# A hybrid decoder layer on one core: sums with one operand in PSUM, and twelve blocks stored alike

## The chip, the cores and the metric

The kernel runs on one core of one Trainium2 chip. The metric is the device time of one execution in microseconds; the median of three runs is given. A core has five engines that work side by side, each with a queue of its own that keeps its order: TensorE (matmuls), VectorE and ScalarE (element by element), GpSimd, and SyncE, called SP here, which issues the transfers (DMAs). [...]

## The reference

One decoder layer on x of 1024 tokens by 1024 channels, all in float32:

```python
h = rms_norm(x, norm_pre_mix)
mix = hybrid_mixer(h, ...)              # RWKV-7 heads beside a causal convolution
x = x + rms_norm(mix, norm_post_mix)
h = rms_norm(x, norm_pre_ffn)
hid = causal_dwconv(h @ ffn_up, ffn_conv_w, ffn_conv_b)   # 3 taps; 1024 -> 2 x 2816
gate, up = hid[..., :2816], hid[..., 2816:]
f = (gelu(gate) * up) @ ffn_down                           # 2816 -> 1024
out = x + rms_norm(f, norm_post_ffn)
```

The change lies in the part from `h @ ffn_up` to the product of gelu(gate) and up.

## The kernel before

The tokens are worked on in two halves of 512. A product of matrices keeps float32's accuracy by splitting both operands into a high part (a rounded copy) and a low part (the rest), and adding three matmuls: high x high, high x low, low x high. For a weight of 128 x 512 ScalarE casts the high part (`wh`), and GpSimd subtracts to get the low part (`wl`); both happen in `split`, line 162. Two buffers each hold `wh` and `wl`, three hold the raw weight (`wr`).

The 2816 channels of the feed-forward part are 22 blocks of 128, each with a gate and an up branch. `project` makes one branch of one block and half of the tokens: 24 matmuls with two weights into one PSUM bank. `taps` applies the three taps of the convolution: ScalarE's scaled copy (line 887) and two VectorE instructions that read the bank and add to an SBUF tile (line 896). `ffn_pair` makes both branches, gelu (line 906) and the product (line 908).

The work goes in this order:

- The mixer, for both halves. Beside its end the first 12 blocks of the first half are made (`EARLY`). They must be kept until the down projection, so they go to DRAM (`early`). Of the 12, the first 8 (`KEPT`) are held in `row` tiles of SBUF, two blocks a tile, and the text stores them at the head of the feed-forward part (line 1196); the last 4 are stored from `pt` tiles where they are made (line 1371).
- `gates`: the gate branches of the last 10 blocks (`JOINT`) of the first half, with the second half's normalisation beside them.
- The plain pairs (lines 1204 to 1206): the first 12 blocks (`PLAIN`) of the second half, one `ffn_pair` each, the result stored to `plain`. `beside` puts next to each pair one step of `weight_sums` (four GpSimd sums, line 1041, with their loads and stores) and one step of `act_sums`, which makes sums and differences of the two halves' activations: four rounds of two steps.
- The joint blocks (`shared`, lines 1210 and 1211): the last 10 blocks for both halves, in a scheme that needs five products in place of six and uses those sums.
- `ffn_down`, the down projection, by a similar scheme with seven products in place of eight, and the output.

From the feed-forward part on, six PSUM banks are handed out in turn (`self.bank()`); two more have the tags "pn" and "pn2" and serve the normalisation and, at the end, the down projection. Within `act_sums` three SBUF tiles x, y and z of the pool `f2p` (six tiles) hold the sums of a round.

The order of each engine's queue is not written by hand: a planner simulates the kernel and puts the instructions in order by priority and readiness. Weight loads, splits and taps are marked high priority. `beside` adds the rule that on VectorE, GpSimd and SP the extra steps come behind the pair's product, its last low part and its last weight load.

Of the kernel before, what the change touches and what calls it, by code (L numbers as in the profile page):

```python
# [13 lines left out]
F32 = mybir.dt.float32  # L14
F32R = mybir.dt.float32r
BF16 = mybir.dt.bfloat16
AF = mybir.ActivationFunctionType
ALU = mybir.AluOpType
# [4 lines left out]
P = 128  # L23
SEQ = 1024
D = 1024
KT = D // P
HALF = 512
# [11 lines left out]
FT = D_FF // P  # L39
# [10 lines left out]
BUFS = {"v": 2, "gd": 1, "pt": 6, "kk": 1, "l8": 5, "ca": 6, "ck": 6, "r": 2,  # L50
        "mixr": 1, "co": 4, "po": 1, "c": 4, "t2": 2}

EARLY, KEPT = 12, 8

JOINT = 10
PLAIN = FT - JOINT
# [42 lines left out]
class Trunk:  # L99
# [181 lines left out]
    def pair(self, what, pool):  # L281
        return tuple(pool.tile([P, HALF], F32R, tag="h", name=self.nm(what)) for _ in range(2))
# [534 lines left out]
    def setup_ffn(self, ctx):  # L817
        nc, tc = self.nc, self.tc
        pool = lambda name, bufs=1: ctx.enter_context(tc.tile_pool(name=name, bufs=bufs))
        cp = pool("fconst")  # L820

        self.turn = cycle([lambda: self.xs[0], lambda: self.xs[1]]
                          + [lambda t=t: Trunk.bank(self, t) for t in ("pe", "pe", "pb", "pb")])
        self.bank = lambda tag="pb": self.Y if tag == "pn2" else Trunk.bank(self, "pc") if tag == "pn" else next(self.turn)()
        self.nrowp = pool("nrowp")

        self.ap = pool("actp", 2 * (FT - KT) - KEPT)
        self.h1p = pool("h1p", 2 * KT)
        self.tp = pool("tp", 8)
        self.f2p = pool("f2p", 6)  # L830
        self.post_ffn = cp.tile([P, D], F32, name="post_ffn")
        nc.sync.dma_start(self.post_ffn, self.a["post_ffn"].broadcast_to([P, D]))
        self.fcarry = cp.tile([P, 2, FT, 2], F32, name="fcarry")
        self.fss = cp.tile([P, 8, 2], F32, name="fss")
# [63 lines left out]
    def ffn_pair(self, h, hs, i, temp, out=None):  # L898

        nc = self.nc  # L900
        accs = []
        for br in range(2):
            ps = self.project(self.a["ffn_up"][br * FT + i], P, hs)
            accs.append(temp())
            self.taps(h, i, br, ps, accs[br])
        nc.scalar.activation(accs[0], accs[0], AF.Gelu_apprx_tanh)
        out = accs[0] if out is None else out
        self.gated = nc.vector.tensor_tensor(out, accs[0], accs[1], ALU.mult)
        return out

    def beside(self, *parts):
# [46 lines left out]
    def act_sums(self, h0, h1, S):  # L958

        nc = self.nc  # L960
        f = lambda t: t.bitcast(F32)
        add = lambda o, x, y: nc.vector.tensor_tensor(o, x, y, ALU.add)
        sub = lambda o, x, y: nc.vector.tensor_tensor(o, x, y, ALU.subtract)

        def pair(n, hi, lo, src):
            self.split(hi, lo, src)
            S[n].append((hi, lo))

        for k in range(4):
            a11, a12, a21, a22 = h0[k], h0[4 + k], h1[k], h1[4 + k]  # L970
            two = [p.tile([P, D], F32R, tag=t, bufs=4, name=self.nm("s")) for p, t in ((self.nrowp, "nrow"), (self.rowp, "row"))]
            x, y, z = (self.f2p.tile([P, HALF], F32, tag="f2", name=self.nm("r")) for _ in range(3))
            whole = lambda out, a: add(out, f(a[0]), f(a[1]))
            whole(z, a11)
            whole(x, a21)
            sub(z, z, x)
            pair(3, *a11, z)
            whole(y, a22)
            add(x, x, y)
            pair(1, two[0][:, :512], two[0][:, 512:], x)  # L980
            yield
            sub(y, y, z)
            pair(2, two[1][:, :512], two[1][:, 512:], y)
            whole(z, a12)
            sub(z, z, y)
            pair(4, *a12, z)
            yield

    def shared(self, i, S, A22, act0, act1, raws):

        nc = self.nc
        temp = lambda: self.f2p.tile([P, HALF], F32, tag="f2", name=self.nm("acc"))
        kview = lambda t: t.rearrange("p (k m) -> p k m", k=4)
        up = self.a["ffn_up"]

        def add(out, x, y):
            with self.tc.high_priority():
                nc.vector.tensor_tensor(out, x, y, ALU.add)

        if raws is None:  # L1000
            T = lambda n: self.weight(kview(self.usums[n - 1]), [P, 4, P])
            b22 = lambda: self.weight(up[FT + i, 1], [P, 4, P])
        else:
            with self.tc.high_priority():
                b11, b12, b21, b22r = raws
                for n in (1, 3, 0, 2):
                    self.load = nc.sync.dma_start(kview(raws[n]), up[n % 2 * FT + i, n // 2])
                t3 = self.wp.tile([P, HALF], F32, tag="wr", bufs=3, name=self.nm("t3"))
                self.four_sums(b11, b12, b21, b22r, t3)

            def pair(raw):
                with self.tc.high_priority():
                    hi, lo = (self.wp.tile([P, HALF], F32R, tag=t, bufs=2, name=self.nm(t)) for t in ("wh", "wl"))
                    self.low = self.split(hi, lo, raw, True)[1]
                return kview(hi), kview(lo)

            T = lambda n: pair((b12, b11, t3, b21)[n - 1])
            b22 = lambda: pair(b22r)
        x, y, z = (self.bank() for _ in range(3))
        self.four(x, T(2), S[2], True, True)  # L1020
        add(act1, act1, x)
        self.four(y, T(1), S[1], True, True)
        W = temp()
        add(W, act1, y)
        self.four(z, T(3), S[3], True, True)
        add(x, W, z)
        self.four(y, b22(), S[4], False, True)
        add(y, act1, y)
        self.four(z, T(4), A22, False, True)
        add(z, act1, z)  # L1030
        two = [temp() for _ in range(2)]
        self.taps(0, i, 1, y, two[0])
        nc.vector.tensor_tensor(act0, act0, two[0], ALU.mult)
        self.taps(1, i, 0, z, act1)
        nc.scalar.activation(act1, act1, AF.Gelu_apprx_tanh)
        self.taps(1, i, 1, x, two[1])
        nc.vector.tensor_tensor(act1, act1, two[1], ALU.mult)

    def four_sums(self, b11, b12, b21, b22, t3):

# [138 lines left out]
    def run(self):  # L1179
        nc = self.nc  # L1180
        self.setup()
        sts = [{}, {}]
        with ExitStack() as ctx:
            self.setup_mixer(ctx)
            h0, early = self.mixer(sts)
        with ExitStack() as ctx:
            self.setup_ffn(ctx)
            h1 = []
# [3 lines left out]
            sums = self.weight_sums()  # L1192
            temp = lambda: self.f2p.tile([P, HALF], F32, tag="f2", name=self.nm("acc"))
            act = lambda: self.ap.tile([P, HALF], F32, tag="act", name=self.nm("act"))
            for i, e in enumerate(early[:KEPT]):
                nc.sync.dma_start(self.early[i], e)
            one = [self.ffn_pair(0, h0, i, temp, act()) for i in range(EARLY, PLAIN)]
            both = [[act() for _ in range(JOINT)] for _ in range(2)]
            turn = cycle((True, False))
# [3 lines left out]
            ss = self.act_sums(h0, h1, S)  # L1203
            for i in range(PLAIN):
                nc.sync.dma_start(self.plain[i], self.ffn_pair(1, h1, i, temp))
                self.beside(sums, ss)
            list(ss)
            list(sums)
            raws = [self.h1p.tile([P, HALF], F32, tag="h", name=self.nm("b")) for _ in range(8)]
            for n, i in enumerate(range(PLAIN, FT)):  # L1210
                self.shared(i, S, h1[4:], both[0][n], both[1][n], raws[n % 2 * 4:n % 2 * 4 + 4] if n else None)
            kept = []
            for i in range(0, KEPT, 2):
                two = self.row("row", 4)
                nc.sync.dma_start(two.rearrange("p (i t) -> p i t", i=2), self.early[i:i + 2].rearrange("i p t -> p i t"))
                kept += [two[:, :HALF], two[:, HALF:]]
            back = [self.hp.tile([P, HALF], F32, tag="h", name=self.nm("act")) for _ in range(2 * KT)]
            for i in range(KEPT, EARLY):
                nc.sync.dma_start(back[PLAIN + i - KEPT], self.early[i])
            for i in range(PLAIN):  # L1220
                nc.sync.dma_start(back[i], self.plain[i])
            acts = [kept + back[PLAIN:] + one + both[0], back[:PLAIN] + both[1]]
# [2 lines left out]
    def mixer(self, sts):  # L1225
        nc, tc = self.nc, self.tc
# [84 lines left out]
        with self.stream("norm"):  # L1311
            two = [self.tl("l8", [P, 2, D]) for _ in range(2)]
# [3 lines left out]
            hs = self.pairs("h")  # L1316
# [21 lines left out]
        hs = self.pairs("h")  # L1338
# [23 lines left out]
        conv(1, 2, W[3].mark)  # L1362
        conv(1, 3)
        conv_norm(1)
        early = []
        with self.stream("proj"):
            piece = lambda: self.tl("pt", [P, HALF])
            for i in range(EARLY):
                if i >= KEPT:
                    early.append(self.early[i])  # L1370
                    nc.sync.dma_start(early[-1], self.ffn_pair(0, h0, i, piece))
                    continue
                if i % 2 == 0:
                    two = self.row("row", 4)
                early.append(self.ffn_pair(0, h0, i, piece, two[:, i % 2 * HALF:(i % 2 + 1) * HALF]))
        prepare(4)
        with self.stream("proj"):
            self.w_out(1, mixes[1], [sts[1]["co", i] for i in range(4)], W[3].merged)
        return h0, early


def pack(ins):
# [70 lines left out]
```

## Time and profile before

| | |
|---|---|
| median of three runs | 1309.98 us (1307.91 to 1310.06) |
| profiled execution | 1311.76 us |
| its span | 1310.0 us |
| TensorE (PE) busy | 1242.8 us, 95% of the span |
| VectorE (DVE) busy | 923.4 us, 70% |
| ScalarE (ACT) busy | 721.5 us, 55% |
| GpSimd (POOL) busy | 508.2 us, 39% |
| granted TensorE clock, mean | 0.979 of full speed |

The span is the time from the first to the last instruction that the profiler saw on the core. Busy shares are means over stages with different limits: a stage's own limit is read from the windows of that stage. [...]

### The profile page before, as it was taken

To read this page: it belongs to the slowest core of one execution; us is meant where nothing else is said; L and a number is where in the kernel's file an instruction comes from. 1 tells how busy PE (TensorE), PEld (TensorE's weight loads), DVE (VectorE), ACT (ScalarE), POOL (GpSimd) and SP (SyncE) were. 2 spreads that over 40 slices of the span, in tenths; PEclk is the share of its full clock that TensorE was granted. 3 is DMA by queue.
4 is the path that set the end of the run, shared out by engine and by line. 5 is a ranking of instruction groups with operands and counts; after the bars stand their busy time and mean duration, and the time that the engine had idled before them with its cause. 6 is when DMAs were issued, how large, how long until landed. Compare 5 with 4: busy or idle time off the path is not lost.

```text
span 1310.0 us, 23010 instructions
## 1 busy us (share of the span) xinstructions
PE 1242.8 (95%) x8460; PEld 998.3 (76%) x8460; DVE 923.4 (70%) x1540; ACT 721.5 (55%) x1490; POOL 508.2 (39%) x438
## 2 busy tenths in 40 slices
PE   6999989999999989999999999889999999999996
PEld 5777767787779867778799777666877888888885
DVE  5276998996689979996520556776366768479567
ACT  6563664657655755557642475545545555544451
POOL 4443420110113422444464388887588860000001
PEclk9999989999999979999999999998999999999998
DMA  7554433343333451332354777676522236335326
GB/s 237 166 153 129 130 98 102 95 140 111 115 112 106 127 172 35 97 89 82 113 155 140 256 267 272 233 250 220 173 57 73 81 120 218 97 105 163 110 65 209
DMA packets 105505, 185.70 MB, mean 142 GB/s; under 512 B 15184, under 2 KB 21712, under 8 KB 105392
## 3 DMA queue, kind: packets, MB, share of 16 engines
q1 hardware_dynamic: 105392, 184.23, 44.1%
q8 instruction: 67, 1.10, 0.3%
q14 instruction: 46, 0.38, 0.1%
HBM read 141.58 MB, written 42.60 MB: 141 GB/s over the span
## 4 chain that ended last, share of the span: by engine, by line
PE 54%; DVE 7%; POOL 4%; DMA 3%; issue 3%; ACT 2%; SPq 0%; POOLq 0%; ACTq 0%
PE pb L135 24%; PE pe L135 14%; PE xs L135 11%; POOL b L1041 2%; DVE pc L416 2%; PE Y L135 2%; PE pc L135 2%; POOL wl L162 2%; DMA wr<-ffn_up 1%; DMA x<-x1d 1%; DVE nrow L1096 1%; DMA nrow<-x 1%; PE pc L150 1%; DVE x L1080 0%; DMA pt<-mixd 0%
## 5 line engine op out<-in xcount | busy, mean ns | idle before, releaser
L162 POOL TENSOR_TENSOR wl<-wr,wh 128x512 fp32r<-128x512 f32 (+1 forms) x181 | 244.5, 1352 | 262.4 <-ACT wh L162 233.6
L162 ACT CAST wh<-wr 128x512 fp32r<-128x512 f32 (+1 forms) x220 | 135.2, 615 | 180.3 <-issue 43.9
L135 PE MATMUL pb<-h,wh 128*128 128x512 f32 (+3 forms) x720 | 229.5, 398 | 2.5 <-ACT wh L162 1.0
L135 PE MATMUL pb<-f,wh 128*128 128x512 f32 x584 | 186.3, 399 | 4.4 <-ACT wh L162 3.3
L416 DVE SCALAR_TENSOR_TENSOR pc<-c,params,pc 128x512 f32<-128x512 f32 x232 | 174.2, 751 | 8.1 <-ACT pc L413 4.1
L135 PEld LDWEIGHTS pb<-h,wh 128*128 128x128 f32 (+2 forms) x720 | 131.7, 188 | 35.1 <-ACT wh L162 2.7
L135 PE MATMUL pb<-h,wl 128*128 128x512 f32 (+3 forms) x360 | 146.3, 406 | 2.2 <-POOL wl L162 2.1
L135 PEld LDWEIGHTS pb<-f,wh 128*128 128x128 f32 x584 | 109.7, 190 | 29.7 <-ACT wh L162 4.8
L135 PE MATMUL pb<-f,wl 128*128 128x512 f32 x292 | 117.6, 403 | 3.2 <-POOL wl L162 3.2
L135 PE MATMUL pe<-f,wh 128*128 128x512 f32 x312 | 99.8, 401 | 2.9 <-ACT wh L162 2.8
L157 POOL TENSOR_TENSOR ss<-var,mhalf 128x1 f32<-128x1 f32 x16 | 11.0, 693 | 227.6 <-DVE ss L1077 202.7
L1041 POOL TENSOR_TENSOR b<-b,b 128x512 f32<-128x512 f32 x66 | 92.9, 1410 | 3.3 <-DMA b<-ffn_down 1.9
L135 PE MATMUL xs<-f,wh 128*128 128x512 f32 x272 | 86.8, 401 | 2.5 <-ACT wh L162 2.1
L135 PEld LDWEIGHTS pb<-h,wl 128*128 128x128 f32 (+2 forms) x360 | 67.6, 188 | 20.6 <-POOL wl L162 4.4
L135 PEld LDWEIGHTS pe<-f,wh 128*128 128x128 f32 x312 | 59.5, 192 | 17.0 <-ACT wh L162 4.0
L135 PEld LDWEIGHTS pb<-f,wl 128*128 128x128 f32 x292 | 55.7, 191 | 17.5 <-POOL wl L162 5.7
L135 PE MATMUL pe<-f,wl 128*128 128x512 f32 x156 | 63.4, 407 | 2.6 <-POOL wl L162 2.6
L135 PEld LDWEIGHTS xs<-f,wh 128*128 128x128 f32 x272 | 51.5, 191 | 14.8 <-ACT wh L162 2.5
L896 DVE SCALAR_TENSOR_TENSOR pt<-pb,params,pt 128x511 f32<-128x511 f32 (+1 forms) x48 | 35.7, 744 | 31.7 <-ACT ecarry L889 31.2
L135 PE MATMUL xs<-f,wl 128*128 128x512 f32 x136 | 54.6, 401 | 1.9 <-POOL wl L162 1.9
L162 POOL TENSOR_TENSOR wl<-b,wh 128x512 fp32r<-128x512 f32 x36 | 47.0, 1306 | 22.4 <-ACT wh L162 18.6
L706 POOL TENSOR_TENSOR XG<-r,GE 64x256 f32<-64x256 f32 x30 | 20.5, 685 | 88.5 <-DVE r L725 83.7
(402 smaller groups left out, 2901.9 us busy)
## 6 DMA issues: line engine op xcount, KB each, us to landing
wr<-ffn_up SPq DMA_DIRECT2D x117, 256.0 KB, 2.8
wr<-w_in SPq DMA_DIRECT2D x80, 256.0 KB, 2.9
b<-ffn_down SPq DMA_DIRECT2D x44, 256.0 KB, 4.4
sums<-b SPq DMA_DIRECT2D x44, 256.0 KB, 2.8
wr<-sums SPq DMA_DIRECT2D x44, 256.0 KB, 2.7
lows<-wl SPq DMA_DIRECT2D x40, 256.0 KB, 3.3
wl<-lows SPq DMA_DIRECT2D x40, 256.0 KB, 2.7
b<-ffn_up SPq DMA_DIRECT2D x40, 256.0 KB, 2.7
```

Of the source, the lines that this page charges most:

```text
L135: return self.nc.tensor.matmul(out, lhsT, rhs, start=start, stop=stop, skip_group_check=skip)
L150: self.nc.tensor.transpose(out, in_, self.con("ident")[:n, :n])
L157: self.nc.gpsimd.tensor_tensor(out, v[:, :n], self.mhalf[:, :n], ALU.pow)
L162: return self.nc.scalar.copy(hi, src), eng.tensor_tensor(lo, src, hi.bitcast(F32), ALU.subtract)
L416: nc.vector.scalar_tensor_tensor(out, c[:, j:j + HALF], w(j), acc, ALU.mult, ALU.add)
L706: nc.gpsimd.tensor_tensor(x[64:128], R[64:128, gs], w.GE[64:128, c, gs].unsqueeze(2).broadcast_to([64, 4, CH]), ALU.mult)
L896: nc.vector.scalar_tensor_tensor(acc[:, o:], ps[:, :HALF - o], w(j), acc[:, o:], ALU.mult, ALU.add)
L1041: sub = lambda o, x, y, op=ALU.subtract: self.nc.gpsimd.tensor_tensor(o, x, y, op)
L1096: nc.vector.tensor_tensor(out, a, b, op)
```

## The change

In `act_sums` the tiles x, y and z become PSUM banks: the two tagged ones and one in turn, and a second one in turn for the last sum of a round. A whole sum (high part plus low part) is now a ScalarE copy of the low part into the bank and a VectorE addition of the high part to it. Where two sums are joined, ScalarE first copies one out of PSUM to an `f2p` tile. So no VectorE instruction here has two inputs in SBUF. A round has three steps in place of two, and every third plain pair gets two steps. In `ffn_pair` of the second half, and at the end of `shared`, gelu writes to a PSUM bank that was already tapped, and the product reads it there. The mixer's twelve blocks are all written to `row` tiles and stored in the mixer, each right behind its product in the text; `KEPT` goes. The pool `actp` keeps 20 tiles.

```diff
-EARLY, KEPT = 12, 8
+EARLY = 12
...
-        self.ap = pool("actp", 2 * (FT - KT) - KEPT)
+        self.ap = pool("actp", 2 * JOINT)
...
     def ffn_pair(self, h, hs, i, temp, out=None):
-        accs = []
+        pss, accs = [], []
         for br in range(2):
-            ps = self.project(self.a["ffn_up"][br * FT + i], P, hs)
+            pss.append(self.project(self.a["ffn_up"][br * FT + i], P, hs))
             accs.append(temp())
-            self.taps(h, i, br, ps, accs[br])
-        nc.scalar.activation(accs[0], accs[0], AF.Gelu_apprx_tanh)
+            self.taps(h, i, br, pss[br], accs[br])
+        gate = pss[0] if h else accs[0]
+        nc.scalar.activation(gate, accs[0], AF.Gelu_apprx_tanh)
         out = accs[0] if out is None else out
-        self.gated = nc.vector.tensor_tensor(out, accs[0], accs[1], ALU.mult)
+        self.gated = nc.vector.tensor_tensor(out, gate, accs[1], ALU.mult)
...
-            x, y, z = (self.f2p.tile([P, HALF], F32, tag="f2", name=self.nm("r")) for _ in range(3))
-            whole = lambda out, a: add(out, f(a[0]), f(a[1]))
+            def whole(out, a):
+                nc.scalar.copy(out, f(a[1]))
+                add(out, f(a[0]), out)
+
+            def copy(src):
+                r = self.f2p.tile([P, HALF], F32, tag="f2", name=self.nm("r"))
+                nc.scalar.copy(r, src)
+                return r
+
+            x, y, z = self.bank("pn"), self.bank("pn2"), self.bank()
             whole(z, a11)
             whole(x, a21)
-            sub(z, z, x)
+            r = copy(x)
+            sub(z, z, r)
             pair(3, *a11, z)
             whole(y, a22)
-            add(x, x, y)
+            add(x, r, y)
+            sub(y, y, copy(z))
+            yield
             pair(1, two[0][:, :512], two[0][:, 512:], x)
+            pair(2, two[1][:, :512], two[1][:, 512:], y)
             yield
-            sub(y, y, z)
-            pair(2, two[1][:, :512], two[1][:, 512:], y)
+            z = self.bank()
             whole(z, a12)
-            sub(z, z, y)
+            sub(z, z, copy(y))
             pair(4, *a12, z)
             yield
...
         self.taps(1, i, 0, z, act1)
-        nc.scalar.activation(act1, act1, AF.Gelu_apprx_tanh)
+        nc.scalar.activation(z, act1, AF.Gelu_apprx_tanh)
         self.taps(1, i, 1, x, two[1])
-        nc.vector.tensor_tensor(act1, act1, two[1], ALU.mult)
+        nc.vector.tensor_tensor(act1, z, two[1], ALU.mult)
...
-            for i, e in enumerate(early[:KEPT]):
-                nc.sync.dma_start(self.early[i], e)
...
                 nc.sync.dma_start(self.plain[i], self.ffn_pair(1, h1, i, temp))
-                self.beside(sums, ss)
+                self.beside(sums, *[ss] * (2 if i % 3 == 0 else 1))
...
             for i in range(EARLY):
-                if i >= KEPT:
-                    early.append(self.early[i])
-                    nc.sync.dma_start(early[-1], self.ffn_pair(0, h0, i, piece))
-                    continue
                 if i % 2 == 0:
                     two = self.row("row", 4)
-                early.append(self.ffn_pair(0, h0, i, piece, two[:, i % 2 * HALF:(i % 2 + 1) * HALF]))
+                nc.sync.dma_start(self.early[i], self.ffn_pair(0, h0, i, piece, two[:, i % 2 * HALF:(i % 2 + 1) * HALF]))
```

## Rows read from the trace of the kernel before

**Rows 1.** The page: busy time by engine, and the chain that ended last.

```profile
PE 1242.8 (95%) x8460; PEld 998.3 (76%) x8460; DVE 923.4 (70%) x1540; ACT 721.5 (55%) x1490; POOL 508.2 (39%) x438
...
PE 54%; DVE 7%; POOL 4%; DMA 3%; issue 3%; ACT 2%; SPq 0%; POOLq 0%; ACTq 0%
```

**Rows 2.** Windows: length, busy us and instructions by engine, clock, DMA share, GB/s.

```profile
784.90:806.70 21.80, 21.80 (x94) 17.47 (x94) 11.83 (x13) 11.72 (x25) 18.07 (x14) 1.00 0.80 270
806.70:907.50 100.80, 88.18 (x339) 66.65 (x338) 76.99 (x80) 53.34 (x109) 82.55 (x58) 0.93 0.69 240
907.50:941.50 34.00, 33.98 (x145) 27.04 (x144) 13.56 (x15) 19.07 (x40) 18.79 (x15) 1.00 0.51 160
...
765.00:780.00 15.00, 15.00 (x74) 12.34 (x73) 8.66 (x17) 9.09 (x21) 12.44 (x11) 1.00 0.90 317
971.00:1085.00 114.00, 113.96 (x490) 91.25 (x489) 79.41 (x112) 65.35 (x138) 87.68 (x67) 1.00 0.32 100
```

**Rows 3.** TensorE's timeline at the start of pair 4: start, us, instructions, wait.

```profile
836.16 0.73 PE L135 MATMUL xs<-f,wh 128*128 128x512 f32 x2 [2.11 <-ACT wh L162]
...
838.05 0.99 PE L135 MATMUL xs<-f,wh 128*128 128x512 f32 x2
...
842.38 0.64 PE L135 MATMUL xs<-f,wh 128*128 128x512 f32 x2
```

**Rows 4.** GpSimd: low halves before and after 806.7 us (ns min/median/max), two timeline rows.

```profile
L162 POOL TENSOR_TENSOR wl<-wr,wh x8: 1288/1306/1737, 783.4 to 802.0; 128x512 fp32r<-128x512 f32 x8
...
L162 POOL TENSOR_TENSOR wl<-wr,wh x29: 1256/1463/1790, 807.8 to 906.6; 128x512 fp32r<-128x512 f32 x29
...
791.99 2.67 POOL L1041 TENSOR_TENSOR b<-b,b 128x512 f32<-128x512 f32 x2
...
818.30 3.44 POOL L1041 TENSOR_TENSOR b<-b,b 128x512 f32<-128x512 f32 x2
```

**Rows 5.** VectorE's groups with both inputs in SBUF: busy us, mean ns, idle before.

```profile
L962 DVE TENSOR_TENSOR r<-f,f 128x512 f32<-128x512 f32 x16 | 22.1, 1418 | 0.1
...
L908 DVE TENSOR_TENSOR acc<-acc,acc 128x512 f32<-128x512 f32 x12 | 14.3, 1195 | 1.2
L963 DVE TENSOR_TENSOR r<-r,r 128x512 f32<-128x512 f32 x12 | 13.7, 1140 | 0.0
...
L1037 DVE TENSOR_TENSOR act<-act,acc 128x512 f32<-128x512 f32 x10 | 11.6, 1162 | 1.8 <-ACT act L1035 1.8
...
L162 DVE TENSOR_TENSOR f<-r,f 128x512 fp32r<-128x512 f32 x8 | 8.3, 1032 | 0.0
...
L962 DVE TENSOR_TENSOR r<-r,r 128x512 f32<-128x512 f32 x4 | 6.7, 1668 | 0.1
...
L162 DVE TENSOR_TENSOR s<-r,s 128x512 fp32r<-128x512 f32 x8 | 5.8, 731 | 0.0
```

**Rows 6.** VectorE: line 896 from 806 to 907 us, and groups of lines 1096 and 998.

```profile
L896 DVE SCALAR_TENSOR_TENSOR acc<-xs,params,acc x12: 734/748/751, 806.4 to 896.8; 128x511 f32<-128x511 f32 x6, 128x510 f32<-128x510 f32 x6
...
L1096 DVE TENSOR_TENSOR act<-act,act 128x512 f32<-128x512 f32 x17 | 11.3, 691 | 0.0
...
L998 DVE TENSOR_TENSOR pe<-act,pe 128x512 f32<-128x512 f32 x10 | 6.9, 690 | 8.1 <-PE pe L135 8.1
```

**Rows 7.** ScalarE's groups: SBUF to SBUF, PSUM to SBUF, SBUF to PSUM.

```profile
L162 ACT CAST wh<-wr 128x512 fp32r<-128x512 f32 x216 | 133.3, 618 | 172.2 <-issue 40.4 <-PE pb L135 38.2 <-POOL wl L162 31.3
...
L556 ACT COPY ck<-pe 128x512 f32<-128x512 f32 x16 | 9.0, 589 | 3.3 <-PE pe L150 3.3
...
L743 ACT ACTIVATE pe<-mixr 128x512 f32<-128x512 f32 x8 | 4.8, 603 | 0.8 <-DVE mixr L742 0.8
```

**Rows 8.** SP's stores of the early blocks, and VectorE's product of block 7.

```profile
L1196 SPq DMA_DIRECT2D early<-row x8: 326/327/327, 523.1 to 631.5; - x8
...
L1371 SPq DMA_DIRECT2D early<-pt x4: 326/326/327, 642.8 to 678.0; - x4
...
630.75 0.68 DVE L908 TENSOR_TENSOR row<-pt,pt 128x512 f32<-128x512 f32 x1
```

More of the change, by code (lines that the diff above doesn't have):

```diff
@@ L1184, in run @@
             self.setup_mixer(ctx)
-            h0, early = self.mixer(sts)
+            h0 = self.mixer(sts)
         with ExitStack() as ctx:
@@ L1212, in run @@
             kept = []
-            for i in range(0, KEPT, 2):
+            for i in range(0, 8, 2):
                 two = self.row("row", 4)
@@ L1217, in run @@
             back = [self.hp.tile([P, HALF], F32, tag="h", name=self.nm("act")) for _ in range(2 * KT)]
-            for i in range(KEPT, EARLY):
-                nc.sync.dma_start(back[PLAIN + i - KEPT], self.early[i])
+            for i in range(8, EARLY):
+                nc.sync.dma_start(back[PLAIN + i - 8], self.early[i])
             for i in range(PLAIN):
@@ L1364, in mixer @@
         conv_norm(1)
-        early = []
         with self.stream("proj"):
@@ L1378, in mixer @@
             self.w_out(1, mixes[1], [sts[1]["co", i] for i in range(4)], W[3].merged)
-        return h0, early
+        return h0
 def pack(ins):
```

## The prediction

> **What bounds the kernel now.** I read the page first. TensorE is busy 95% of the span, and over half of the chain of work that ended last is matmuls, with a few per cent each for VectorE, GpSimd and the rest [rows 1]. So an edit is worth something only where TensorE stands still or runs at its lower clock. Next I cut the feed-forward part into windows at the start times of TensorE's groups. The twelve plain pairs of the second half run from 784.9 to 941.5 us; a pair is 48 matmuls. Pairs 9 to 11 fill 34.00 us without a gap, 11.33 each, and pairs 0 and 1 are as dense. Between them pairs 2 to 8 take 100.80 us, where seven at 11.33 would take 79.3. **So 21.5 us are lost in this stretch**, and the window splits them: TensorE is idle for 100.80 - 88.18 = 12.6 us, and its busy time is 8.9 more than 79.3, at a mean granted clock of 0.93 [rows 2]. TensorE's timeline shows both: the first matmuls of a weight wait 2.1 us for the cast weight, and the ones behind them take 0.99 us for two where 0.64 is normal [rows 3].
>
> What is late is GpSimd. For each pair it makes four low halves (line 162) and four weight sums (line 1041). In the clean stretch a low half takes 1.31 us in the median and two sums in a row 2.67; in the lossy one 1.46 (up to 1.79) and 3.44 [rows 4]. The windows agree: 82.55 us for 58 instructions, 1.42 each, against 18.07 / 14 = 1.29 [rows 2]. What the lossy stretch has and the clean ones lack is VectorE's work on the sums of activations, and those instructions are slow on VectorE too: means of 0.73 to 1.67 us [rows 5]. All of them take both inputs from SBUF. In the same stretch VectorE's taps, with one input in PSUM, keep to 0.73-0.75; the additions of line 998, one input in PSUM, keep to 0.69 beside GpSimd's work; and a two-input SBUF sum in the last part, where GpSimd rests, takes 0.69 as well [rows 6]. So VectorE with two SBUF inputs and GpSimd hold each other up, and with one input in PSUM they don't.
>
> **The change, part by part.**
>
> Sums of activations (act_sums) and the plain pairs' gated products. A round has four whole sums, one addition, three subtractions and four low halves: 48 VectorE instructions in four rounds, and 12 products, in all 22.1 + 6.7 + 13.7 + 8.3 + 5.8 + 14.3 = 70.9 us for 60 [rows 5]. Each now has one input in PSUM, at 0.69 [rows 6]: 41.4 us. The 29.5 us that VectorE gets back are off the path by themselves; what counts is GpSimd. Freed, its eight instructions of a pair take 8 x 1.3 = 10.4 us, less than TensorE's 11.3; held up, 8 x 1.42 = 11.4 were more. Its queue has two sums ahead of a low half now and then. Unhindered: a weight's buffer comes free, cast 0.62, low half 1.3, two sums 2.6, the next low half 1.3, about 5.9 us with the hand-overs. That low half is needed two weights (2 x 11.33 / 4) and two matmuls (0.47) later, at 6.1. It just fits; with 1.79 and 3.44 instead it is over a microsecond late, which is the wait seen. And where TensorE doesn't stop, there is nothing here that lowers the clock: 1.00 in both clean stretches [rows 2]. Most that this can give: 21.5 us; least: nothing, if the lateness has another cause.
>
> What it adds is ScalarE work: per round four copies into PSUM and three out of it, 28 in all. A copy out of PSUM takes 0.59, a write into it 0.60, SBUF to SBUF 0.62 [rows 7]: 28 x 0.61 = 17.1 us. ScalarE's load without sums is 19.07 / 3 = 6.4 us a pair (pairs 9 to 11). The twelve steps are now spread over pairs 0 to 8, so nine pairs carry 9 x 6.4 + (28 + 16 casts) x 0.61 = 84 us in 102 us, 83%, where it was 53% [rows 2]. Two steps at once put 8 or 9 such instructions beside pairs 0 and 6, 4.9 to 5.5 us on top of 6.4: a full pair. Behind a copy stands the cast of the next weight, and TensorE waits for that. Bounds: nothing, if every cast passes first; above, one copy in front of each of the 36 casts of nine pairs, 36 x 0.62 = 22 us, the whole gain. The stretch nearest to the new one, pairs 0 and 1, with weight sums and half of ScalarE's time taken, shows no TensorE wait. I take 3 us, five delays of one copy, nearer to that end, since a sixth of ScalarE's time stays free and casts are marked high priority.
>
> [...]
>
> Gelu of a plain pair now writes the first projection's bank. Its write stays near 0.6 us. The bank is held until the second projection is tapped, some 6 us longer (24 matmuls). Six banks rotate, two for a pair and two for a round of sums, so it is wanted again after two pairs at the earliest. Nothing; a bank that is late after all costs what it is late.
>
> Joint phase: ten products of line 1037 go from 1.16 to 0.69 us [rows 5], 4.7 us of VectorE. From 971 to 1085 us TensorE is busy 113.96 of 114 us [rows 2], so this wins nothing. The sums of activations end one pair later, which leaves some two pairs before the first joint block reads them. Nothing.
>
> The mixer's twelve blocks. Eight stores move from the head of the feed-forward part into the mixer, on SP's queue, where weight loads stand behind them. But before, too, they went out early: between 523.1 and 631.5 us, one at a time, the last within 0.1 us of the end of its product (630.75 + 0.68) [rows 8]. Their number, size and moment stay, and the other four came from the mixer already, from 642.8 us on. Those now take a row buffer; the buffers they get were stored many tens of us earlier. Nothing; at worst 0.33 us of issue for each of eight, 2.6 us.
>
> DMA: a pair in 11.33 us moves 13 transfers of 256 KB, 3.4 MB, at 301 GB/s. Between 765 and 780 us 317 GB/s went through with TensorE busy 15.00 of 15 us [rows 2]. Nothing.
>
> Sum: -21.5 + 3 = **-18.5 us**. The profiled execution took 1311.76 us around a span of 1310.0; it would go to 1293.3. It lies 1.8 us above the median of the runs, and from the median the forecast is 1309.98 - 18.5 = **1291.5 us**.
>
> **Rivals.**
>
> A, ScalarE is fuller than hoped: its copies wait for VectorE's results in a queue that keeps its order, and the casts behind them are late. For it: 83% load. Against: casts that waited for VectorE stood in that queue before. If 18 of the 36 weights lose 0.62 us, 11 us go: 1309.98 - 21.5 + 11 = 1299.5.
>
> B, GpSimd is late by its order and not by the hold-ups: two sums ahead of a low half stay, and a margin of 0.2 us is thin. Against: such a pair of sums at 791.99 [rows 4] cost TensorE nothing. Then only 58 x 0.13 = 7.5 us of GpSimd's time come back, half of it where TensorE waits: 1306.
>
> C, the other side: the copies stop ScalarE itself. Each of the 28 can find VectorE in two taps of 0.75 us [rows 6] and hold its queue for 1.5 us, 0.9 more than one instruction there takes. All of them so: 28 x 0.9 = 25 us, and 1309.98 - 21.5 + 25 = 1313.5. It decides from 21.5 / 28 = 0.77 us per copy. Against: that all hit a pair of taps.
>
> D, the planner lays the mixer's queues otherwise and the row buffers bind. Nothing in the rows asks for it; the eight stores at 0.33 us and one row buffer waited for over a third of a pair (4 us) give 1291.5 + 6.6 = 1298.
>
> **How the numbers follow.** Forecast 0.65, with a range of its own of 1287 to 1296 (from the full gain, with 1.5 us more at the joints, to 7.5 us lost on ScalarE); A 0.18; B 0.06; C 0.06; D 0.05. About 0.2%, 2.6 us, is what a measurement of this kernel can tell from no change. Faster: forecast, A, D and two thirds of B, 0.92. Same: the rest of B and a little of C, 0.03. Slower: the rest of C, 0.05. The range runs from 1286 through A and D to 1303; C and B stay out.
>
> **What would show it.** Right: low halves and sums at 1.27-1.31 us throughout the plain loop, act_sums and products at 0.69, the twelve pairs in 136 to 140 us, a granted clock of 1.00. Wrong: TensorE waits for casts that stand behind a copy of act_sums (A, C); waits for low halves while GpSimd runs at 1.3 (B); a mixer that ends later than before (D).

## The result and the profile after

The changed kernel takes 1290.84 us in the median of four executions (1285.73 to 1292.88), against 1309.11 us (1307.91 to 1310.06) for the kernel before beside it: a ratio of 0.9855, with a 95% interval from 0.9822 to 0.9888. Between the medians that is 18.3 us, where 18.5 was forecast.

The profiled execution of the changed kernel is the fastest of its four: 1285.73 us around a span of 1284.0. The page's busy times and the chain that ended last stand beside [rows 1] like this:

```profile
PE 1229.7 (96%) x8460; PEld 990.3 (77%) x8460; DVE 891.1 (69%) x1540; ACT 731.4 (57%) x1518; POOL 495.8 (39%) x438
...
PE 56%; DVE 7%; DMA 3%; ACT 3%; POOL 2%; issue 2%; SPq 0%; POOLq 0%; ACTq 0%; DVEq 0%
```

The counts of TensorE, VectorE and GpSimd are the same as before; ScalarE has the 28 copies more. VectorE lost 32 us of busy time (923.4 - 891.1), GpSimd 12 (508.2 - 495.8), and GpSimd's share of the chain fell from 4% to 2%. TensorE too is busy for 13 us less with the same 8460 matmuls, and 11 of them go with the clock: its mean over the span rose from 0.979 to 0.988, and 1242.8 x 0.979 / 0.988 = 1231.5.

Windows of the changed kernel come next (columns as in [rows 2]): the unchanged mixer at 400 to 500 and 460 to 480 us, the twelve plain pairs, pairs 1 to 9 about, and a stretch within them.

```profile
400.00:500.00 100.00, 91.58 (x1239) 79.61 (x1239) 90.74 (x182) 67.03 (x164) 31.14 (x32) 0.97 0.43 130
...
460.00:480.00 20.00, 17.11 (x209) 12.84 (x208) 16.14 (x40) 10.91 (x32) 5.32 (x7) 0.93 0.61 199
...
778.10:915.20 137.10, 135.92 (x576) 107.50 (x576) 73.32 (x107) 93.38 (x197) 107.85 (x85) 1.00 0.76 260
...
789.00:890.50 101.50, 100.32 (x424) 78.87 (x423) 62.94 (x93) 74.08 (x157) 87.59 (x70) 1.00 0.85 288
...
828.00:888.00 60.00, 59.68 (x255) 47.30 (x254) 37.42 (x56) 42.80 (x92) 53.35 (x43) 1.00 0.84 295
```

The twelve pairs run from 778.1 to 915.2 us, 137.1 us instead of 156.6 (784.9 to 941.5). Twelve pairs at 11.33 would be 136.0. TensorE is idle for 137.10 - 135.92 = 1.2 us in all of them, at a granted clock of 1.00, where [rows 2] had 12.6 us idle at 0.93 in seven pairs. A GpSimd instruction takes 87.59 / 70 = 1.25 us there, where it was 1.42. The same can be read from GpSimd's two groups between 790 and 900 us (ns: min/median/max):

```profile
L1053 POOL TENSOR_TENSOR b<-b,b x34: 1287/1296/1312, 789.1 to 884.8; 128x512 f32<-128x512 f32 x34
...
L162 POOL TENSOR_TENSOR wl<-wr,wh x39: 1273/1295/1312, 790.3 to 899.0; 128x512 fp32r<-128x512 f32 x39
```

None is above 1.31 us any more, neither low halves nor weight sums; [rows 4] had up to 1.79, and 3.44 for a pair of sums. On VectorE, groups that answer to [rows 5] (busy us, mean ns | idle before); line 964 is the subtraction, 963 the addition, 909 and 1049 are products, and 1045 is the joint block's other product, which the change leaves with two SBUF inputs (`xs`, `Y`, `pb`, `pc` and `pe` are PSUM banks):

```profile
L964 DVE TENSOR_TENSOR Y<-Y,r 128x512 f32<-128x512 f32 x4 | 2.8, 700 | 4.6 <-ACT r L979 4.6
...
L963 DVE TENSOR_TENSOR xs<-f,xs 128x512 f32<-128x512 f32 x4 | 2.7, 686 | 0.0
...
L162 DVE TENSOR_TENSOR s<-Y,s 128x512 fp32r<-128x512 f32 x4 | 2.7, 681 | 0.0
...
L909 DVE TENSOR_TENSOR acc<-xs,acc 128x512 f32<-128x512 f32 x5 | 3.5, 692 | 0.5
...
L1049 DVE TENSOR_TENSOR act<-pb,acc 128x512 f32<-128x512 f32 x5 | 3.4, 689 | 0.7 <-ACT pb L1047 0.3
...
L1045 DVE TENSOR_TENSOR act<-act,acc 128x512 f32<-128x512 f32 x10 | 12.8, 1280 | 0.0
```

Every changed form is at 0.68 to 0.70 us, the unchanged one still at 1.28. What TensorE waits for between 778 and 913 us (total us, times, longest) is short:

```profile
PE pb L135 <- POOL wl L162: 0.5, 1, 0.5
PE xs L135 <- POOL wl L162: 0.3, 1, 0.3
PE pb L135 <- ACT wh L162: 0.2, 1, 0.2
```

**The two profiles differ by more than the kernels do.** They are 26.0 us apart (1311.76 - 1285.73), the medians 18.3. Three groups of stores on SP's queue (the mixer's output, the early blocks, the plain blocks) let the difference be cut by place; after, and then two of before:

```profile
L790 SPq DMA_DIRECT2D mixd<-t x16: 372/377/426, 402.2 to 723.8; - x16
...
L1380 SPq DMA_DIRECT2D early<-row x12: 326/327/327, 518.2 to 671.3; - x12
...
L1215 SPq DMA_DIRECT2D plain<-acc x12: 326/327/419, 793.8 to 920.3; - x12
```

```profile
L790 SPq DMA_DIRECT2D mixd<-t x16: 372/378/1309, 403.6 to 730.2; - x16
...
L1205 SPq DMA_DIRECT2D plain<-acc x12: 319/326/382, 800.5 to 946.6; - x12
```

The mixer's last store starts at 723.8 us, 6.4 us earlier than in the profile of before (730.2). Most of that is not the change's doing. The first instructions that differ are the product and the store of the ninth early block, and 5.8 of the 6.4 us are there by then: the store starts at 642.8 us before [rows 8], at 637.0 after.

```profile
636.99 0.33 SPq L1380 DMA_DIRECT2D early<-row  x1
```

Up to there each engine runs the same instructions in the same order. In one stretch of 20 us among them the kernel before had

```profile
460.00:480.00 20.00, 17.01 (x196) 11.90 (x197) 12.23 (x32) 9.30 (x28) 4.82 (x6) 0.76 0.58 184
```

so a clock of 0.76 where the other execution was granted 0.93. Four experiments below that keep the old stores (1, 5, 6 and 10) end it at 723.9 to 725.6 us; over all kernels it lies between 721.6 and 730.2, and the profile of before has the latest. Of the rest, 19.7 us lie between the mixer's end and the first joint matmul (211.1 to 191.4 us), and from there to the end the two are alike (368.7 and 368.8). So I measure the change in the plain loop: from its first to its last store 146.1 us before (800.5 to 946.6) and 126.5 after (793.8 to 920.3), **19.6 us less**.

### The profile page after: what moved, and what is told of

Its sections match the earlier page's. It is cut to its first block, busy times and chain, and to the rows that moved or that the text cites. A ratio compares the mean times of both kernels' runs of the same rounds, so it can differ in the third digit from the quotient of the medians.

```text
span 1284.0 us, 23035 instructions
## 1 busy us (share of the span) xinstructions
PE 1229.7 (96%) x8460; PEld 990.3 (77%) x8460; DVE 891.1 (69%) x1540; ACT 731.4 (57%) x1518; POOL 495.8 (39%) x438
## 4 chain that ended last, share of the span: by engine, by line
PE 56%; DVE 7%; DMA 3%; ACT 3%; POOL 2%; issue 2%; SPq 0%; POOLq 0%; ACTq 0%; DVEq 0%
PE pb L135 27%; PE pe L135 13%; PE xs L135 12%; PE Y L135 2%; PE pc L135 2%; DVE pc L416 2%; POOL wl L162 1%; POOL b L1053 1%; DMA x<-x1d 1%; DVE nrow L1108 1%; DMA pt<-mixd 1%; DMA b<-ffn_up 1%; PE pc L150 1%; DMA m<-mixd 1%; PE pe L150 0%
## 5 line engine op out<-in xcount | busy, mean ns | idle before, releaser
L135 PE MATMUL pb<-f,wh 128*128 128x512 f32 x696 | 219.2, 395 | 2.5 <-ACT wh L162 1.5
L135 PEld LDWEIGHTS pb<-f,wh 128*128 128x128 f32 x696 | 129.4, 188 | 32.2 <-ACT wh L162 3.0
L135 PE MATMUL pb<-f,wl 128*128 128x512 f32 x348 | 138.3, 398 | 1.4 <-POOL wl L162 1.4
L135 PE MATMUL pe<-f,wh 128*128 128x512 f32 x272 | 85.5, 395 | 0.1
L135 PEld LDWEIGHTS pb<-f,wl 128*128 128x128 f32 x348 | 65.4, 188 | 17.5 <-POOL wl L162 3.4
L135 PE MATMUL xs<-f,wh 128*128 128x512 f32 x200 | 62.8, 395 | 0.4 <-DVE act L950 0.4
L135 PEld LDWEIGHTS pe<-f,wh 128*128 128x128 f32 x272 | 50.9, 188 | 11.6 <-ACT wh L162 0.3
L135 PE MATMUL pe<-f,wl 128*128 128x512 f32 x136 | 53.9, 397 | 0.7 <-POOL wl L162 0.7
L178 ACT CAST wh<-wr 128x512 fp32r<-128x512 f32 (+2 forms) x44 | 26.5, 604 | 41.2 <-PE pb L135 30.0
L162 ACT CAST wh<-b 128x512 fp32r<-128x512 f32 x36 | 22.2, 617 | 47.4 <-PE pb L135 18.1
```

The lines of the kernel that those rows point to most:

```text
L135: return self.nc.tensor.matmul(out, lhsT, rhs, start=start, stop=stop, skip_group_check=skip)
L162: return self.nc.scalar.copy(hi, src), eng.tensor_tensor(lo, src, hi.bitcast(F32), ALU.subtract)
L178: self.nc.scalar.copy(hi, raw)
```

## The experiments

Ten more kernels were run, each beside the kernel before, to which its ratio is. "Loop" is first to last plain store in the profiled execution, "mixer" the start of the mixer's last store. From the first to the last of twelve stores are eleven pairs: 126.5 us where all twelve took 137.1, so the expectations of 5 and 6, which speak of the whole plain loop, compare with the table plus 10.6 us. Each loop is read from one execution. That of 10 has the same plain pairs as the changed kernel and lasts 3.9 us longer, so a microsecond between two loops says nothing.

| kernel | median us (runs) | ratio to before [95%] | mixer | loop us |
|---|---|---|---|---|
| before | 1309.11 (4) | | 730.2 | 146.1 |
| after | 1290.84 (4) | 0.9855 [0.9822, 0.9888] | 723.8 | 126.5 |
| 1 products alone | 1305.18 (9) | 0.9958 [0.9940, 0.9976] | 725.6 | 140.3 |
| 2 without the products | 1291.96 (4) | 0.9856 [0.9836, 0.9877] | 724.9 | 127.2 |
| 3 stores alone | 1308.65 (12) | 0.9989 [0.9973, 1.0004] | 727.2 | 147.0 |
| 4 sums in SBUF tiles | 1307.12 (12) | 0.9977 [0.9964, 0.9989] | 726.3 | 144.1 |
| 5 no sums of activations | 1289.77 (4) | 0.9842 [0.9807, 0.9877] | 723.9 | 126.4 |
| 6 no weight sums | 1287.20 (4) | 0.9828 [0.9793, 0.9864] | 724.3 | 126.8 |
| 7 half of the rounds | 1298.79 (6) | 0.9905 [0.9877, 0.9933] | 726.2 | 137.4 |
| 8 copies twice | 1290.69 (4) | 0.9848 [0.9812, 0.9884] | 725.5 | 127.2 |
| 9 joint block's other product | 1288.35 (5) | 0.9838 [0.9814, 0.9862] | 721.6 | 126.3 |
| 10 after, old stores | 1292.78 (4) | 0.9873 [0.9853, 0.9893] | 725.5 | 130.4 |

**1. The products alone.** The kernel before with only the second half's Gelu written to the bank:

```diff
...
-        nc.scalar.activation(accs[0], accs[0], AF.Gelu_apprx_tanh)
+        gate = pss[0] if h else accs[0]
+        nc.scalar.activation(gate, accs[0], AF.Gelu_apprx_tanh)
...
-        nc.scalar.activation(act1, act1, AF.Gelu_apprx_tanh)
+        nc.scalar.activation(z, act1, AF.Gelu_apprx_tanh)
```

> Only the products change: gelu writes a PSUM bank in the plain pairs and the joint blocks, and the product reads it there; sums of activations and stores as before. The hold-up theory: 12 of the 60 two-input VectorE instructions of the plain loop are freed, 6.0 us of the 29.5 us by which they are too slow, so about 6.0 / 29.5 of the loop's gain of 19.5 us comes back: 4 us, 1305 (1302 to 1308) against 1309. GpSimd late by its order alone: no change. The ten products of the joint blocks: nothing.

Measured: 1305.18 us, 5.8 us off the loop. The product is quick, the old sums beside it are as slow as ever, and GpSimd takes 106.96 / 76 = 1.41 us an instruction (VectorE groups, then a window of the plain loop):

```profile
L909 DVE TENSOR_TENSOR acc<-xs,acc 128x512 f32<-128x512 f32 x4 | 2.8, 692 | 0.4
...
L964 DVE TENSOR_TENSOR r<-r,r 128x512 f32<-128x512 f32 x12 | 18.1, 1506 | 0.0
```

```profile
783.00:909.00 126.00, 113.18 (x468) 86.25 (x467) 90.48 (x97) 69.10 (x142) 106.96 (x76) 1.00 0.74 253
```

One long two-input instruction less per pair is worth something by itself, but the sums still hold GpSimd.

**2. The change without the products.** Both Gelus of 1 back in place, all else of the change kept:

```diff
-        nc.scalar.activation(gate, accs[0], AF.Gelu_apprx_tanh)
+        nc.scalar.activation(accs[0], accs[0], AF.Gelu_apprx_tanh)
...
```

> The changed kernel with the products put back to two SBUF inputs. The hold-up theory: 48 of the 60 instructions stay freed, the 12 products are held up again at about 1.2 us, so some 4 us are lost to the changed kernel: 1295 (1292 to 1299). If the products' banks or ScalarE were what matters: as the changed kernel or faster.

Measured: 1291.96 us, and a loop only 0.7 us longer than after. I had expected about 4 us of loss; the ratios, 0.9856 and 0.9855, show none. Yet the products are as slow as before (VectorE's group):

```profile
L908 DVE TENSOR_TENSOR acc<-acc,acc 128x512 f32<-128x512 f32 x12 | 15.8, 1314 | 1.2
```

The parts don't add: products alone give 5.8 us of the loop, the rest of the change 18.9, together 19.6. With the sums out of the way, one held-up instruction per pair costs nothing that can be measured.

**3. The stores alone.** The kernel before with the mixer's twelve blocks all stored at once:

```diff
...
-            for i, e in enumerate(early[:KEPT]):
-                nc.sync.dma_start(self.early[i], e)
...
             for i in range(EARLY):
-                if i >= KEPT:
-                    early.append(self.early[i])
-                    nc.sync.dma_start(early[-1], self.ffn_pair(0, h0, i, piece))
-                    continue
                 if i % 2 == 0:
                     two = self.row("row", 4)
-                early.append(self.ffn_pair(0, h0, i, piece, two[:, i % 2 * HALF:(i % 2 + 1) * HALF]))
+                nc.sync.dma_start(self.early[i], self.ffn_pair(0, h0, i, piece, two[:, i % 2 * HALF:(i % 2 + 1) * HALF]))
```

> Only the stores change: the mixer's twelve blocks all go through row tiles and are stored from the mixer. The stores were issued behind their products before, too: no change, 1309 within 2 us, and the mixer's end moves only as it does from one execution to the next. The rival that the 6.4 us by which the mixer ended earlier in the changed kernel's profile come from the stores: 1303.

Measured: 1308.65 us over twelve runs; the interval holds 1. No time can be found in the stores.

**4. The same new steps, with SBUF tiles for the banks.** The copies, their order and the two steps at once stay as in the changed kernel; only x, y and z live in SBUF:

```diff
+        self.sb = pool("sb", 4)
...
-            x, y, z = self.bank("pn"), self.bank("pn2"), self.bank()
+            sb = lambda: self.sb.tile([P, HALF], F32, tag="sb", name=self.nm("q"))
+            x, y, z = sb(), sb(), sb()
...
-            z = self.bank()
+            z = sb()
```

> The changed kernel with x, y and z of the sums of activations in SBUF tiles in place of PSUM banks: the same 28 ScalarE copies, the same three steps, the same instructions in number, but two SBUF inputs on VectorE. The hold-up theory: the 48 instructions are slow again (above 1.0 us in the mean) and the loop loses at least 13 of its 19.5 us: 1303 to 1314. If the new order of the steps or the copies made the gain: 1291 as the changed kernel.

Measured: 1307.12 us, and a loop of 144.1: 17.6 of the 19.6 us are lost again. VectorE's groups, GpSimd's timeline (start, us) and a window of the plain loop:

```profile
L964 DVE TENSOR_TENSOR q<-f,q 128x512 f32<-128x512 f32 x16 | 19.1, 1236 | 0.0
...
L965 DVE TENSOR_TENSOR q<-q,r 128x512 f32<-128x512 f32 x12 | 17.4, 1458 | 0.4
...
L964 DVE TENSOR_TENSOR q<-r,q 128x512 f32<-128x512 f32 x4 | 7.1, 1777 | 0.0
```

```profile
841.67 3.48 POOL L1055 TENSOR_TENSOR b<-b,b 128x512 f32<-128x512 f32 x2
...
850.10 1.75 POOL L162 TENSOR_TENSOR wl<-wr,wh 128x512 fp32r<-128x512 f32 x1
...
854.12 3.45 POOL L1055 TENSOR_TENSOR b<-b,b 128x512 f32<-128x512 f32 x2
```

```profile
779.00:890.00 111.00, 98.80 (x398) 75.70 (x396) 81.89 (x80) 69.45 (x142) 94.40 (x66) 0.97 0.75 258
```

The same instructions in the same order, and with the operand in SBUF they take up to 1.78 us in a group's mean on VectorE, 94.40 / 66 = 1.43 on GpSimd, and TensorE idles 12.2 us of 111. So it is the bank, not the new order, that pays, nor room in `f2p`, since the SBUF tiles here have a pool of their own. In the medians 3 us are still gained (0.9964 to 0.9989), which fits the products, whose bank stays. The edit also makes all of ScalarE's copies SBUF to SBUF, which by [rows 7] is 0.62 us for 0.59 or 0.60.

**5 and 6. One party taken away.** In the kernel before, 5 leaves the sums of activations out, 6 the weight sums on GpSimd (their loads and stores stay):

```diff
...
-            x, y, z = (self.f2p.tile([P, HALF], F32, tag="f2", name=self.nm("r")) for _ in range(3))
...
+            S[3].append(a11)
+            S[1].append(a11)
...
+            S[2].append(a12)
+            S[4].append(a12)
```

```diff
-            self.four_sums(*b, b[3])
```

> The kernel before with the sums of activations left out: the joint blocks read the activations themselves, so none of the 48 VectorE instructions and 16 casts is there; the products keep two SBUF inputs. It leaves out part of the computation. The hold-up theory: only the 12 products can hold GpSimd up, and GpSimd has time for it: the plain loop takes 136 to 139 us and the kernel 1289 to 1292. If it is faster than the changed kernel by more than 3 us, that is what the new copies on ScalarE cost.

> The kernel before with GpSimd's sums of weights left out (their loads and stores stay, the raw weights are stored): it leaves out part of the computation. VectorE's two-input instructions are all there. The hold-up theory: the low halves still take up to 1.8 us, but GpSimd has four instructions a pair instead of eight, and each may be late by 0.5 us without TensorE noticing: the plain loop takes 135 to 139 us, the kernel 1288 to 1293. If VectorE's slowness itself bound the loop: above 150 us and no gain.

Measured: loops of 126.4 and 126.8 us. Whichever of the two is gone, the loss is gone, and the loop comes to the length that it has after the change (126.5). Nothing more was to be had here. 5 keeps all of GpSimd's work and its order; 6 takes half of it away, so by itself 6 doesn't tell the hold-up from a GpSimd with too much to do. In 6 one detail missed its expectation: the low halves that are left are not held up, while VectorE's two-input instructions stay slow (GpSimd's low halves, then VectorE's groups):

```profile
L162 POOL TENSOR_TENSOR wl<-wr,wh x34: 1281/1294/1388, 800.6 to 897.3; 128x512 fp32r<-128x512 f32 x34
```

```profile
L908 DVE TENSOR_TENSOR acc<-acc,acc 128x512 f32<-128x512 f32 x12 | 17.3, 1443 | 1.2
...
L963 DVE TENSOR_TENSOR r<-r,r 128x512 f32<-128x512 f32 x12 | 12.6, 1052 | 0.0
```

**7. Half of the rounds.** The changed kernel with rounds 1 and 3 of the sums, counted from 0, in their old form:

```diff
+            if k % 2:
+                x, y, z = (self.f2p.tile([P, HALF], F32, tag="f2", name=self.nm("r")) for _ in range(3))
+                whole = lambda out, a: add(out, f(a[0]), f(a[1]))
...
+                continue
```

> The changed kernel with two of the four rounds of sums (the second and fourth) in the form before, on SBUF tiles with two steps. The hold-up theory: the loss comes back about in proportion to the 24 instructions: 6 to 11 us, 1297 to 1302. If one freed round were enough for GpSimd to catch up: 1291 to 1293.

Measured: 1298.79 us, a loop of 137.4: 8.7 of the 19.6 us are left, a little under half. With the products already moved, 24 two-SBUF-input instructions put back cost 10.9 us of the loop and 48 (experiment 4) 17.6; the 12 products of 2 cost 0.7. More of them cost more, but not in proportion.

**8. Each copy made twice.** 28 ScalarE instructions more, in the places where rivals A and C saw the danger:

```diff
                 nc.scalar.copy(out, f(a[1]))
+                nc.scalar.copy(out, f(a[1]))
...
                 nc.scalar.copy(r, src)
+                nc.scalar.copy(r, src)
```

> The changed kernel with each of the 28 new ScalarE copies made twice, 17 us more on ScalarE, which the nine pairs then fill to 99%. If the copies find room beside the casts: 2 to 8 us slower than the changed kernel, 1293 to 1299. If each copy stood in front of a cast for which TensorE waits (rival A): 17 us slower, 1308.

Measured: 1290.69 us, a loop of 127.2. I had expected 2 to 8 us of loss; there is none that can be measured. ScalarE's timeline (start, us) and a window over pairs 1 to 9:

```profile
805.66 0.61 ACT L974 COPY xs<-f 128x512 f32<-128x512 f32 x1
806.17 0.61 ACT L975 COPY pc<-f 128x512 f32<-128x512 f32 x1
806.69 0.61 ACT L162 CAST s<-Y 128x512 fp32r<-128x512 f32 x1
```

```profile
791.00:893.50 102.50, 99.99 (x424) 78.73 (x422) 62.28 (x93) 85.80 (x182) 87.70 (x70) 1.00 0.83 285
```

Each lasts 0.61 us, but they start 0.51 to 0.52 apart: one begins before the last has ended. ScalarE is busy 85.80 of 102.5 us, 84%, and TensorE keeps a clock of 1.00.

**9. The joint block's other product.** The changed kernel, and line 1045's product takes one input from a bank too, by a copy:

```diff
-        nc.vector.tensor_tensor(act0, act0, two[0], ALU.mult)
+        nc.scalar.copy(y, two[0])
+        nc.vector.tensor_tensor(act0, act0, y, ALU.mult)
```

> The changed kernel carried one step further: in the joint blocks the other product (line 1045, still two SBUF inputs, 1.28 us in the mean) reads a PSUM bank to which ScalarE has copied the second factor; ten more copies. TensorE loses only 1.35 us at the start of the joint blocks, 0.4 of it to a low half that this product held up: 0 to 0.4 us faster than the changed kernel, 1290 to 1291, not told from it. If held-up GpSimd instructions still cost in the joint blocks: 3 us faster or more.

Measured: 1288.35 us. The product (ns: min/median/max) falls from 1.28 to 0.68 us, but the start of the joint phase is no better:

```profile
L1046 DVE TENSOR_TENSOR act<-act,xs x5: 677/678/684, 929.9 to 1044.5; 128x512 f32<-128x512 f32 x5
```

```profile
914.00:935.00 21.00, 19.37 (x82) 14.55 (x81) 11.12 (x17) 10.14 (x22) 18.09 (x15) 1.00 0.32 105
```

```profile
914.00:935.00 21.00, 19.65 (x82) 14.79 (x81) 11.01 (x16) 10.03 (x21) 17.74 (x15) 1.00 0.36 123
```

TensorE is busy 19.37 of these 21 us, 19.65 in the changed kernel (second window). The median is 2.5 us under that of the changed kernel, but the intervals of the ratios overlap almost wholly, and 2.2 us of its own profile are an earlier end of the mixer (721.6 to 723.8), which this edit does not touch. It is the lowest median of a full kernel here and not told apart from the change.

**10. The change with the old stores.** All of the change except the mixer's stores and buffers, which are as before (the reverse of 3).

> The changed kernel with the stores of the mixer's twelve blocks as before (eight held in row tiles and stored in the text of the feed-forward part, four stored from pt tiles). If the stores are worth nothing: as the changed kernel, 1289 to 1293. If they carry the 6.4 us by which the mixer ended earlier: 1297.

Measured: 1292.78 us, 0.9873 [0.9853, 0.9893], against 0.9855 [0.9822, 0.9888] for the whole change. Its loop of 130.4 us holds one TensorE wait of 1.9 us, for a low half, at a mean clock of 0.97 in the 60 us around it. With 3 this leaves 0 to about 2 us for the stores; whether they are worth anything stays open.

## Why the prediction was right

**What is lost and why.** The forecast took 21.5 us for what pairs 2 to 8 lost, and laid it on VectorE instructions with two SBUF inputs and GpSimd holding each other up. Experiments 4, 5 and 6 show both: take away either party and the loss goes (146.1 to 126.4 and 126.8), or give VectorE the same steps with SBUF operands and it comes back (144.1). The traces show the two taking turns, instruction by instruction (last section). The clock went with TensorE's waits here: in windows of 2 us, before, it fell to 0.53, 0.50 and 0.50 behind the three waits of 2.1 us, which end at 836.2, 864.2 and 892.3 us, and was 1.00 in the rest of the pairs; after, with 1.2 us of idle TensorE, it is 1.00 throughout. That idle time alone lowers it isn't shown: in 1 TensorE was idle for 12.8 us of 126 at a mean of 1.00.

For the same subtraction and sums VectorE's groups take 1.24 to 1.78 us in 4, with both inputs in SBUF, and 0.69 to 0.70 after, with one in a bank.

**VectorE at 0.69.** Right for all sums, low halves and products (0.681 to 0.700).

With GpSimd at rest (no instruction of it from 1160 to 1212 us of before) the two-input form too takes 0.691 us [rows 6]; from a bank it is 0.686 for an addition and 0.692 for a product.

**GpSimd just fits.** Forecast 8 x 1.3 = 10.4 us a pair against TensorE's 11.3, with 0.2 us to spare where two sums stand ahead of a low half. Instructions at 1.295 in the median and two waits of 0.8 us together say that it does. Rival B falls with it, and with 5, where GpSimd's eight instructions a pair keep their order and the loss is gone: the order alone costs no more than those 0.8 us. 6 says nothing on B, since it takes away the two sums as well.

**ScalarE: the term that was mis-sized most.** The prediction took 3 us for casts that are late behind a copy. TensorE's waits in the loop come to 1.0 us, and 0.2 of it is for a cast. So the loop gained 19.5 us (156.6 to 137.1) where 18.5 was forecast, inside the 136 to 140 us named for twelve pairs. The other term was about 1 us too large: pairs 0 and 1 took 21.80 us [rows 2] where two at 11.33 are 22.7, so part of their work fell into the window of pairs 2 to 8, and all twelve pairs had 156.6 - 136.0 = 20.6 us to win, not 21.5. Of these 1.1 did not come, not 3. The load was mis-sized with it: 74.08 / 101.50 = 73%, not 83%. I had multiplied 44 instructions by 0.61 us each, as if they stood one behind the other. In the window from 789.0 us on, 424 matmuls are 8.83 pairs; at 40 / 3 = 13.3 instructions and 6.36 us a pair without sums [rows 2], 157 - 118 = 39 instructions and 74.08 - 56.2 = 17.9 us are left, 0.46 us each. The busy time counts overlapping stretches once, and back to back these instructions overlap (8: 0.61 us each, 0.51 to 0.52 apart). Experiment 8 brought ScalarE to 84% and still lost nothing, so rival A falls whatever the load was. Rival C falls with it: a copy of a round does wait for VectorE now and then, as one of two ScalarE groups between 778 and 915 us shows (on the right the idle time before all of a group, and what ended it),

```profile
L974 ACT COPY xs<-f 128x512 f32<-128x512 f32 x3 | 1.8, 599 | 0.0
...
L979 ACT COPY r<-pc 128x512 f32<-128x512 f32 x4 | 2.3, 583 | 1.3 <-DVE pc L963 1.3
```

but that is one wait of 1.3 us, and all of this line's twelve copies out of a bank waited 1.6 us together, far from the 0.77 a copy from which it would have decided.

**The edits costed at nothing.** Stores: 3 and 10 put them between 0 and 2 us in the change's favour, none against; rival D falls, since the mixer's last store starts at 721.6 to 727.2 us with the new stores and at 723.9 to 730.2 with the old. Joint products: from 971 us on nothing was won, as said (368.7 against 368.8 us from the first joint matmul), and 9 shows the same for the other product. DMA: 295 GB/s from 828 to 888 us, with TensorE busy for 59.68 of 60 us.

**What went right by luck.** The cause and the signs named for it were right; that 1291.5 us meets 1290.84 so closely is luck. One term was 2 us too dear and the other promised 1 us too much, so their errors partly cancel, and the four executions of the changed kernel lie up to 7.2 us apart (1285.73 to 1292.88).

## What to carry to other kernels

Before moving work off an engine, look for instructions that last longer in one stretch than elsewhere with the same shape: here VectorE at 1.2 to 1.8 us for 0.69 and GpSimd at up to 1.79 for 1.29 named the pair that held each other up, and one operand moved to a PSUM bank freed both (0.68 to 0.70 and 1.27 to 1.31 after). Pay for it on an engine that overlaps its own instructions, as ScalarE did here (0.61 us each, started 0.51 to 0.52 apart), and judge its load by starts, not by summed durations. Parts that relieved the same bottleneck didn't add here (5.8 and 18.9 us of the loop alone, 19.6 together), so test each alone and each left out, and compare the stretch as well as the total: two executions of the same instructions differed here by nearly 6 us ahead of the change.

## What was not expected of the hardware

- The hold-up goes by turns: whichever of the two starts second ends a nearly fixed time after the first, as these rows of the kernel before (start, us) and the counts below them show:

```profile
825.42 1.29 POOL L1041 TENSOR_TENSOR b<-b,b 128x512 f32<-128x512 f32 x1
...
825.53 1.72 DVE L908 TENSOR_TENSOR acc<-acc,acc 128x512 f32<-128x512 f32 x1
...
826.67 1.74 POOL L162 TENSOR_TENSOR wl<-wr,wh 128x512 fp32r<-128x512 f32 x1
```

The product starts while a weight sum runs and ends 0.54 us after it; the low half starts while the product runs and ends 1.16 us after that. The rest of the loop is the same. Of VectorE's 60 instructions the 35 that start while GpSimd works end 0.54 to 0.55 us after GpSimd's instruction, whatever was left of it, and last 0.89 to 1.79; the other 25 last 0.67 to 0.69. Of GpSimd's, 35 start during one of those 60 and end 1.13 to 1.21 us after it; the others last 1.26 to 1.32.
- So the hold-up isn't shared evenly. With only low halves left on GpSimd (experiment 6) these took 1.29 us, while VectorE's products took 1.44 instead of 0.69; with the weight sums too (before, and 4) both suffer. In 6 GpSimd has pauses:

```profile
806.87 1.29 POOL L162 TENSOR_TENSOR wl<-wr,wh 128x512 fp32r<-128x512 f32 x1 [2.40 <-ACT wh L162]
810.24 1.29 POOL L162 TENSOR_TENSOR wl<-wr,wh 128x512 fp32r<-128x512 f32 x1 [2.08 <-ACT wh L162]
```

```profile
806.91 1.79 DVE L963 TENSOR_TENSOR r<-r,r 128x512 f32<-128x512 f32 x1
```

VectorE's instruction ends 0.54 us after one low half (808.70 against 808.16) and is over 1.5 us before the next starts. The 34 low halves of 6 between 800 and 900 us last 1.388 us at most.
- Two of ScalarE's 128x512 copies and a cast in a row (experiment 8, from 805.66 us) last 0.61 us each and start 0.51 to 0.52 us apart, so a sum of durations overstates its load there by a fifth (0.61 / 0.51).
- The same mixer instructions ran at a granted clock of 0.76 in one execution and 0.93 in another (460 to 480 us), before the first instruction that the change alters.
